# One query block of layer 0 scored once, queries on partitions, with DMA-turned weights

## The chip, the core and the metric

The kernel runs on one NeuronCore of a Trainium2 chip. Five engines work in parallel, each through its own queue of instructions in order: TensorE (PE, matmuls; PEld is its weight load), VectorE (DVE), ScalarE (ACT), GpSimd (POOL) and SyncE (SP), which here only starts DMA transfers. Engines wait for one another through semaphores. The metric is the device time of one execution in microseconds; the number to be predicted is the median of several executions.

## The reference, cut to what matters

Two layers over 1024 latent tokens and 256 context tokens of width 1024. Layer 0 is multi-head latent attention with 16 heads, layer 1 is differential attention with 8 head pairs. The change touches layer 0's attention only:

```python
def one_block(qb):                                   # q: 64 plain + 32 rotary columns a head
    s = jnp.einsum('bqhgd,bkhd->bhgqk', qb, k).astype(jnp.float32) * scale
    p = jax.nn.softmax(s, axis=-1).astype(v.dtype)
    return jnp.einsum('bhgqk,bkhv->bqhgv', p, v)

# latent queries see latent and context keys, context queries only context keys
o = dense_attention(q, concat([k, k_c]), concat([v, v_c]), scale)
o_c = dense_attention(q_c, k_c, v_c, scale)
```

Inputs are float32. The kernel keeps the precision by splitting operands into a high and a low half (float16 in the attention, a rounded float32 in the projections) and summing three products: high by high, high by low, low by high.

## The kernel before, in words

Before layer 0's attention the kernel computes modulation, input projections and gates (to about 222 us), and after it the output projection with layer norm, then layer 1 (from about 925 us) and its output.

Layer 0's attention is the function `heads0`. Each head has three chunks of queries (`CHUNKS`): b=0 is tokens 0 to 511, b=1 is tokens 512 to 1023, b=2 is the 256 context tokens. For a head and a chunk two things are done.

- `maxima0` finds a bound for the softmax. With queries on partitions it computes the high-by-high scores of each 128-query tile against all 1024 latent keys (`m.mm`, two matmuls of 512 columns into a PSUM pair, line 931), takes the row maximum on DVE (`m.max`, line 935), does the same for the 256 context keys (`m.mmc`, `m.maxc`, lines 942 and 947), joins both (`m.ng`), turns the 128 x 4 maxima into rows by a small matmul (`m.turn`, line 953) and writes them as four extra rows of the query tile `qH` (`m.row`, line 956). The key tile has the constant 16 in those rows, so a matmul over 100 rows subtracts the bound by itself.
- `attend0` computes the scores again, this time with keys on partitions and all three products (`s.mm`, six matmuls of 512 columns a unit, lines 980 to 982). A unit is two key tiles by 512 queries, one PSUM pair of 128 x 1024. Five units make a chunk (four of latent keys, one of context keys). ACT takes the exponential (`s.exp`, L986) and casts to float16 (`s.hi`, L988), POOL subtracts to get the low half (`s.lo`, L990), and because keys are on partitions the weights are already laid out for the second product: `pv.hi` (L998, L999) and `pv.lo` (L1005) add into one PSUM bank of kind "d" that is held for the whole chunk. Then DVE divides by the sum (`o.rc`, `o.out`, L1013, L1014) and SP stores the heads' output.

So the high-by-high product of every query chunk is computed twice, once in each orientation.

The PSUM holds three pairs (kind "a") for scores, maxima and projections, and two banks (kind "d") for results. The order of the work is written out by a planner (class `Plan`): each piece is a task with an engine, an estimated cost, buffers that it reads, writes and takes new, and a priority, which is a place on a scale of 11 units a head (`a`) plus an offset for its kind (`OFF0`). The planner runs the tasks through a model of the engines, picks on each engine among the tasks that could start first (within `EPS0`) the one of lowest priority, and looks no further than `AHEAD0` units ahead. The resulting order is what each engine's queue executes, SP's included. A new buffer of a kind takes the oldest of a ring: the n-th buffer back has to be free.

Around the heads: `query_move` and `key_move` bring a head's queries and keys to partitions 0 to 95 by SBUF-to-SBUF DMAs on SP (line 119; four transfers a query chunk, two for the keys). `key_pair`, `query_pair` and `turned` project for two or four heads at once and take the staging tiles `stk*`, `stq*`, `stp*`, `rsw`, `rr`. `range1` (lines 1025 to 1050, in head 2) computes layer 1's scale from small vectors, on DVE and with two small matmuls (L1035). `out_w0` loads the eight row blocks of the output weight in heads 14 and 15 into the two `ows` tiles and splits them (L1066 to L1068). In the last head the context chunk goes first, so that the context tokens' output projection (`ctx_turn`, `ctx_half`, L1092 and L219 to L221) can follow the last scores on PE.

Layer 1 treats a tile of 128 queries in another way, which is of use below: scores once with queries on partitions, maximum on DVE, the bound as the bias of the exponential (L1887), a cast and a subtraction (L1905, L1906), and then two DMA transposes on SP (`far.move`, L1909) that put keys on partitions for the second product (L1809 to L1811).

Of the kernel before, what the change touches and what calls it, by code (L numbers as in the profile page):

```python
# [14 lines left out]
ALU = mybir.AluOpType  # L15
# [18 lines left out]
PB = (3, 4)  # L34
# [28 lines left out]
OFF0 = {"c.hi": -13.45, "c.lo": -225.35, "c.load": 1.9, "c.mm": 1.45, "c.mul": -306.3, "c.turn": -151.55, "h.ab":  # L63
       26.55, "h.mm": -70.9, "h.three": 48.15, "h.two": -80.0, "k.hi": -179.3, "k.lo": 6.35, "k.mm": -8.55,
       "k.move": -44.05, "keep": -65.25, "m.max": -11.25, "m.maxc": -38.85, "m.mm": -1.15, "m.mmc": -1.55, "m.ng":
       -157.1, "m.row": -55.4, "m.turn": -102.05, "o.out": -258.15, "o.rc": -53.05, "o.store": -100.35, "open":
       -81.95, "p.add": 7.75, "p.c.hi": -140.45, "p.c.lo": -123.0, "p.cos": -56.4, "p.hi": -40.35, "p.lo": -17.55,
       "p.mm": -4.65, "p.mmc": 0.95, "p.sin": -19.1, "p.swap": -162.2, "pv.hi": 1.8, "pv.lo": 1.65, "q.hi": -104.55,
       "q.lo": -126.15, "q.mm": -5.3, "q.move": -151.4, "s.exp": -36.65, "s.hi": -13.6, "s.lo": -137.8, "s.mm":
       -0.75, "v.hi": 9.4, "v.lo": -112.0, "v.mm": -2.1, "v.out": 11.15, "v.sub": -65.0, "w.hi": 22.9, "w.lo":  # L70
       -226.85, "w.load": -135.85}
EPS0 = dict(P=0.0, A=0.0, D=0.15, G=0.3)
AHEAD0 = 30.25
# [13 lines left out]
def hybrid_kernel(  # L87
# [35 lines left out]

    def pair():

        return banks["pool"].tile([P, 1024], F32, tag="a", bufs=banks["a"], name=nm("ps_a"))
# [25 lines left out]
    ksc0, qsc0, esc0, sh0 = (col(1, s_) for s_ in ("ksc0", "qsc0", "esc0", "sh0"))  # L152
    ones = col(P, "ones")
# [267 lines left out]
    def up_weights(pa):  # L421
# [84 lines left out]
        dve.scalar_tensor_tensor(sh0, ksc0, math.log(4.0) / SC0, qsc0, op0=ALU.mult, op1=ALU.mult)  # L506
        kh_, kl_ = (u().bitcast(F16)[:ROPE, :NTOK] for _ in range(2))
# [93 lines left out]
    with spool("p0g") as pg:  # L601
# [18 lines left out]
        for _ in chain(gw, side):  # L620
# [13 lines left out]
            "qcL": ([100, 256], F16, 2), "op": ([P, NT, P], F32, 1), "mx": ([P, 4, 3], F32, 2),  # L634
            "ng": ([P, 4], F32R, 2), "rc": ([P, 4], F32, 2), "rsw": ([P, 1024], F32, 1), "rr": ([P, 1024], F32, 1),
            "stkH": ([P, NTOK], F16, 1), "stkL": ([P, NTOK], F16, 1), "stqH": ([P, NTOK], F16, 1),
            "stqL": ([P, NTOK], F16, 1), "stpH": ([P, NTOK], F16, 1), "stpL": ([P, NTOK], F16, 1),
            "ows": ([P, D], F32, 2), "cs": ([P, SEQ], F32, 2)}
    for k_, v_ in TAG0.items():
        rot(wk, v_[0], v_[1], k_, v_[2], first=True)  # L640
# [3 lines left out]
    rot(wk, *TAG0["p32"][:2], "p32", PB[0], first=True)  # L644

    def w0(tag, dt=None):
        sh, d, b = TAG0[tag]
        return rot(wk, sh, d, tag, b)

    cosA, sinA = w0("cs"), w0("cs")  # L650
# [38 lines left out]
    class Plan:  # L689
# [39 lines left out]

        def run(self, eps, ahead):  # L730
# [12 lines left out]
            order = []  # L743
            while done < len(T):
                best = None
                low = min(t["pri"] for l in ready.values() for t in l)
                for lim in (ahead, 1e9):
                    if best is not None:
                        break
                    for e, l in ready.items():  # L750
                        c = []
                        for t in l:
                            if t["pri"] > low + lim and t["pri"] > self.step + lim:
                                continue
                            st = max(free[e], t["at"])
                            if e == "G" or (e, t["kind"]) in self.PORT:
                                st = max(st, port)
                            for j, b in enumerate(t["new"]):
                                n, ring = self.rings[b.tag]
                                n -= sum(x.tag == b.tag for x in t["new"][:j])  # L760
                                if len(ring) >= n:
                                    for u in ring[-n].users:
                                        if u["end"] is None:
                                            st = None
                                            break
                                        st = max(st, u["end"] + self.LAT)
                                    if st is None:
                                        break
                            if st is not None:
                                c.append((st, t))  # L770
# [11 lines left out]
                for b in t["new"]:  # L782
                    self.rings[b.tag][1].append(b)
# [17 lines left out]
    def make0(tag):  # L801
        return pair() if tag == "a" else bank("d") if tag == "d" else w0(tag)
# [3 lines left out]
    def heads0():  # L806
# [3 lines left out]
        pl_ = Plan(rings, OFF0)  # L810
        add = pl_.add
# [151 lines left out]
        def attend0(h, b, a):  # L963
            c0, n = CHUNKS[b]
            QH, QLo = QT[h, b]
            kcs = list(range(0 if b < 2 else SEQ // P, NT, 2))
            nt = n // P
            nr = DQ + nt
            i = h % 2
            pv = new1("d")  # L970
            x = n == 512
            v_ = lambda: pv.tile[:, :4 * (V0 + 1)].rearrange("p (t d) -> p t d", t=4)
            for u, kc in enumerate(kcs):
                st, p32, ph, pl = new1("a"), new1("p32"), new1("ph"), new1("pl")

                def scores(kc=kc, st=st):
                    for j in range(2):
                        ks = slice((kc + j) * P, (kc + j + 1) * P)
                        s_ = st.tile[:, j * n:(j + 1) * n]
                        pe.matmul(s_, KH[i][:nr, ks], QH.tile[:nr, :], start=True, stop=False)  # L980
# [1152 lines left out]
```

## Time and profile before

| | us |
|---|---|
| median of 3 runs (1637.2 to 1639.33) | 1637.84 |
| profiled execution | 1638.62 |
| its span in the trace | 1636.8 |
| PE busy in the span | 1560.9 (95%) |
| DVE, ACT, POOL busy in the span | 1172.6, 1099.1, 1061.9 |
| PE's first and last score matmul of layer 0's attention (L980 start, L982 start) | 253.4, 721.4 |

The busy times are sums over instructions of one engine. PE's matmuls are pipelined, so that a busy PE can still have a few per cent to give; the exact cost of one more matmul in a full stretch is read from the chain of waits, where two matmuls of 512 columns take 0.43 us. "Chain" is the chain of work that ended last: followed back from the end, each instruction or the one that released it. Only what stands on it can shorten the kernel. The windows view gives for stretches of the span the busy time of each engine, PE's granted clock (1.00 is full speed) and the share of time in which the 16 DMA engines were busy.

### The profile page before, as it was taken

Reading aid. Unit: us, or ns where it says so; the run is one execution under the profiler, and the core shown is the slowest. Engines: PE = TensorE matmul, PEld = TensorE weight load, DVE = VectorE, ACT = ScalarE, POOL = GpSimd, SP = SyncE. Lnnn points to the kernel's source line nnn. Section 1 sums busy time; section 2 is a strip of 40 time slices with the busy share of each in tenths; the row PEclk is TensorE's granted clock in tenths of the full one; section 3 lists DMA queues with packets and bytes.
Section 4 is the critical chain, followed back from the end, with each engine's and each line's share of the span. In section 5 each row is a group of like instructions: output and inputs, shape, how many; then the busy total and the mean of one; then the engine's idle time right before and its main releaser. Section 6 shows DMA issues by size and latency. Waiting matters only on the chain.

```text
span 1636.8 us, 35530 instructions
## 1 busy us (share of the span) xinstructions
PE 1560.9 (95%) x13860; PEld 1135.9 (69%) x13860; DVE 1172.6 (72%) x1904; ACT 1099.1 (67%) x2074; POOL 1061.9 (65%) x816
## 2 busy tenths in 40 slices
PE   7999989999999999999999899999999999996998
PEld 6999965566666666667886576667676757574686
DVE  7757846776676676864774688888888888876763
ACT  2652147678878888974553678787878788867651
POOL 2513126767867877884556376877878687866794
PEclk9999999999999999999999999999999999997999
DMA  9347730111111102316443366667465666575772
GB/s 326 93 135 226 221 110 13 31 43 39 51 27 45 51 22 79 107 50 241 154 142 102 77 131 143 136 143 154 111 142 119 133 134 121 121 173 133 178 181 81
DMA packets 280438, 193.07 MB, mean 118 GB/s; under 512 B 181607, under 2 KB 255943, under 8 KB 280270
## 3 DMA queue, kind: packets, MB, share of 16 engines
q1 hardware_dynamic: 272398, 183.46, 44.2%
q10 hardware_dynamic: 7872, 7.34, 1.3%
q8 instruction: 109, 1.79, 0.5%
q14 instruction: 59, 0.48, 0.1%
HBM read 98.65 MB, written 27.07 MB: 77 GB/s over the span
## 4 chain that ended last, share of the span: by engine, by line
PE 65%; DVE 16%; DMA 5%; POOL 5%; ACT 5%; issue 3%; SPq 0%; POOLq 0%; DVEq 0%; ACTq 0%
PE ps_s L219 5%; PE ps_s L221 5%; PE ps_s L220 5%; PE ps_a L980 4%; PE ps_a L981 4%; PE ps_a L982 4%; PE ps_a L219 3%; PE ps_a L221 3%; PE ps_a L931 3%; PE ps_a L220 3%; DVE mx L1876 3%; DMA pd<-dl 2%; PE ps_d L998 2%; DVE p L1900 2%; PE ps_d L1005 2%
## 5 line engine op out<-in xcount | busy, mean ns | idle before, releaser
L990 POOL TENSOR_TENSOR pl<-p,ph 128x1024 f16<-128x1024 f32 (+1 forms) x176 | 362.1, 2076 | 113.7 <-ACT ph L988 79.3
L986 ACT ACTIVATE p<-ps_a,esc 128x1024 f32<-128x1024 f32 (+1 forms) x176 | 188.7, 1074 | 57.3 <-PE ps_a L982 42.8
L935 DVE TENSOR_REDUCE mx<-ps_a 128x1 f32<-128x1024 f32 x128 | 156.2, 1223 | 81.8 <-PE ps_a L931 81.1
L1906 POOL TENSOR_TENSOR dl<-p,dh 128x1280 f16<-128x1280 f32 x64 | 171.7, 2683 | 54.9 <-ACT dh L1905 35.5
L988 ACT CAST ph<-p 128x1024 f16<-128x1024 f32 (+1 forms) x176 | 176.5, 1006 | 9.7 <-PE ps_d L999 5.0
L1876 DVE TENSOR_REDUCE mx<-ps_p 128x1 f32<-128x512 f32 x256 | 163.9, 681 | 19.6 <-PE ps_p L1860 19.4
L1887 ACT ACTIVATE p<-ps_p,mx 128x512 f32<-128x512 f32 x256 | 173.3, 689 | 0.0
L1811 PE MATMUL ps_t<-vh,pd 128*128 128x128 f16 x640 | 113.2, 222 | 19.5 <-DMA pd<-dl 19.5
L980 PE MATMUL ps_a<-qH,KH 100*128 100x512 f16 x320 | 122.4, 382 | 2.1 <-ACT op L833 1.5
L981 PE MATMUL ps_a<-qH,KL 96*128 96x512 f16 x320 | 121.9, 381 | 0.0
L982 PE MATMUL ps_a<-qL,KH 96*128 96x512 f16 x320 | 121.0, 378 | 0.0
L1905 ACT CAST dh<-p 128x1280 f16<-128x1280 f32 x64 | 80.5, 1258 | 54.4 <-DVE p L1900 27.7
L1809 PE MATMUL ps_t<-vh,pd 128*128 128x128 f16 x640 | 113.8, 222 | 0.0
L1810 PE MATMUL ps_t<-vl,pd 128*128 128x128 f16 x640 | 113.6, 222 | 0.0
L1900 DVE SCALAR_TENSOR_TENSOR p<-p,sm,p 128x1280 f32<-128x1280 f32 x64 | 103.4, 1615 | 3.2
L998 PE MATMUL ps_d<-Vh,ph 128*128 128x65 f16 x1344 | 105.1, 195 | 0.0
L999 PE MATMUL ps_d<-Vl,ph 128*128 128x64 f16 x1344 | 104.6, 194 | 0.0
L998 PEld LDWEIGHTS <-ph 128*128 128x128 f16 x1344 | 90.3, 98 | 10.5 <-issue 5.3
L999 PEld LDWEIGHTS <-ph 128*128 128x128 f16 x1344 | 88.2, 98 | 4.5
L1887 ACT ACTIVATE p<-ps_c,mx 128x256 f32<-128x256 f32 x128 | 60.7, 474 | 33.7 <-DVE mx L1881 27.6
L1854 PE MATMUL ps_p<-KS,QS 128*128 128x512 f16 x256 | 77.2, 388 | 3.0 <-ACT p L1887 1.7
L1811 PEld LDWEIGHTS <-pd 128*128 128x128 f16 x640 | 63.5, 99 | 21.7 <-DMA pd<-dl 21.7
(496 smaller groups left out, 5115.9 us busy)
## 6 DMA issues: line engine op xcount, KB each, us to landing
ws<-in_dw SPq DMA_DIRECT2D x28, 512.0 KB, 4.9
adw<-in_ada_w SPq DMA_DIRECT2D x24, 512.0 KB, 4.7
adaw<-in_ada_w SPq DMA_DIRECT2D x16, 512.0 KB, 7.2
g<-sg_d SPq DMA_DIRECT2D x16, 512.0 KB, 4.4
sg_d<-gg ACTq DMA_DIRECT2D x40, 128.0 KB, 3.2
o_d<-op SPq DMA_DIRECT2D x7, 640.0 KB, 3.7
xt<-in_xT SPq DMA_DIRECT2D x16, 256.0 KB, 3.8
wgs<-in_w_in SPq DMA_DIRECT2D x32, 128.0 KB, 3.0
```

The costliest lines, as they stand in the source:

```text
L980: pe.matmul(s_, KH[i][:nr, ks], QH.tile[:nr, :], start=True, stop=False)
L981: pe.matmul(s_, KL[i][:DQ, ks], QH.tile[:DQ, :], start=False, stop=False)
L982: pe.matmul(s_, KH[i][:DQ, ks], QLo.tile[:DQ, :], start=False, stop=True)
L986: add("s.exp", "A", 1.114 if x else 0.682, lambda st=st, p32=p32: act.activation(p32.tile[:, :2 * n], st.tile[:, :2 * n], AF.Exp, scale=esc0),
L988: add("s.hi", "A", 1.046 if x else 0.618, lambda p32=p32, ph=ph: act.copy(ph.tile[:, :2 * n], p32.tile[:, :2 * n]), r=[p32], new=[ph], hol ...
L990: add("s.lo", "G", 2.14 if x else 1.17, lambda p32=p32, ph=ph, pl=pl: pool.tensor_tensor(pl.tile[:, :2 * n], p32.tile[:, :2 * n], ph.tile[ ...
L998: pe.matmul(v_()[:, t, :], w, Vh[:, k, h, :], start=(k == kcs[0] and t == 0), stop=False, skip_group_check=True)
L999: pe.matmul(v_()[:, t, :V0], w, Vl[:, k, h, :], start=False, stop=False, skip_group_check=True)
L1811: pe.matmul(pt.tile[:, :P], b, vh.tile[:, kc, :], start=False, stop=kc == NT - 1)
L1876: add(f"max{m}", "D", 0.68, lambda i=i, b_=b_: dve.tensor_reduce(mx.tile[:, 2 + 2 * m + i:3 + 2 * m + i], b_.tile, axis=AX.X, op=ALU.max, ...
L1887: add(f"exp{m}", "A", 0.78 if n == 512 else 0.57, lambda i=i, c0=c0, n=n, b=b, lo=lo: act.activation(p[m].tile[:, c0:c0 + n], b.tile[:, lo ...
L1906: add("far.lo", "G", 2.63, lambda: pool.tensor_tensor(dl.tile, p[0].tile, dh.tile, op=ALU.subtract), r=[p[0], dh], new=[dl], at=g + PR["fa ...
```

## The change

For chunk b=1 of each head the two functions are replaced by one, `mixed0`. For each of its four 128-query tiles it computes all three products once with queries on partitions (`x.mm`, six matmuls of 512 columns into a pair), takes the negated maximum (`x.max`), forms a bias of two small DVE instructions (`m.bias`), and takes the exponential with that bias (`x.exp`), the cast (`x.hi`) and the subtraction (`x.lo`) as before. Then two DMA transposes on SP (`s.turn0`, `s.turn1`) put the high and the low half, 128 x 1024 float16 each, with keys on partitions into one of the tiles `ows`, `rr`, `rsw`, and PE adds them into the result bank (`x.pvh`, `x.pvl`, as many matmuls as before). The context keys of the chunk are still done the other way round in one unit (`unit0`), with the bound written as rows of `qH` (`x.ng`, `x.trn`, `x.row`); their maximum (`x.mmc`, `x.maxc`, `m.cr`) now comes first.

Chunks b=0 and b=1 now alternate through the head (step 2.0 for both); before, b=0 came first. Layer 0's tiles and its PSUM pairs and banks get a tag for each buffer, and the planner picks among those that are free (`place`). There are five buffers of `ph` and `pl` in place of four, four of `mx`, three of `ng`. The output weight is loaded for all eight blocks in head 14 into `rr`, `rsw` and `cs`, after the point `open`, and the context loads (`c.load`) come after its splits. The planner's costs for `range1` rise (1.3 to 4.9, 0.52 to 1.1, 0.7 to 1.0), and all offsets, `EPS0` and `AHEAD0` (30.25 to 12.75) have new values.

```diff
-PB = (3, 4)
+PB = (3, 5)
-EPS0 = dict(P=0.0, A=0.0, D=0.15, G=0.3)
-AHEAD0 = 30.25
+EPS0 = dict(P=0.1, A=0.1, D=0.05, G=0.1)
+AHEAD0 = 12.75
...
+        def place(self, new):
+            st, taken = 0.0, []
+            for j, b in enumerate(new):
+                n, ring = self.rings[b.tag]
+                if self.pick:
+                    free = []
+                    for k, old in enumerate(self.held[b.tag]):
+                        us = old.users if old is not None else ()
+                        if (b.tag, k) not in taken and all(u["end"] is not None for u in us):
+                            free.append((max([u["end"] + self.LAT for u in us], default=0.0), k))
+                    if not free:
+                        return None
+                    at, k = min(free)
...
+        PDT = "ows", "rr", "ows", "rsw"
+        def mixed0(h, b, a, step=1.0):
...
+            add("x.mmc", "P", 4 * C(CTX), g, r=[(QH, "q"), KB[i]], new=[ps], at=a - 0.5)
+            add("x.maxc", "D", 1.223, lambda: dve.tensor_reduce(
+                mx.tile[:, :, 1], ps.tile.rearrange("p (a b) -> p a b", a=4), axis=AX.X, op=ALU.max, negate=True),
+                r=[ps], new=[mx], hold=1.255, at=a - 0.3)
+            add("m.cr", "D", 0.32, ctx_rows, w=[mx], new=[r16], hold=0.2, at=a - 0.25)
+            for t in range(4):
+                st, p32, ph, pl, pd = new1("a"), new1("p32"), new1("ph"), new1("pl"), new1("ows" if last else PDT[t])
+                def scores(st=st, ts=ts):
+                    for w, ks, first, stop in ((QH, KH, True, False), (QH, KL, False, False), (QLo, KH, False, True)):
+                        for c in range(2):
+                            pe.matmul(st.tile[:, c * 512:c * 512 + 512], w.tile[:DQ, ts], ks[i][:DQ, c * 512:c * 512 + 512], start=first, stop=stop)
+                def bias(t=t):
+                    dve.tensor_scalar(r16.tile[:, t:t + 1], mx.tile[:, t, 0:1], 1.0 / MROW0, sh0m, op0=ALU.mult, op1=ALU.add)
+                    dve.tensor_scalar(mx.tile[:, t, 2:3], r16.tile[:, t:t + 1], mx.tile[:, t, 1:2], esm0, op0=ALU.min, op1=ALU.mult)
...
+                add("x.exp", "A", 1.114, lambda t=t, st=st, p32=p32: act.activation(p32.tile, st.tile, AF.Exp, bias=mx.tile[:, t, 2:3], scale=esc0),
+                    r=[st, (mx, ("b", t))], new=[p32], hold=1.0, at=a + step * t + 0.3)
...
+                for j, d in enumerate((ph, pl)):
+                    add(f"s.turn{j}", "S", 3.4, lambda j=j, d=d, vw=vw: sp.dma_start_transpose(vw()[:, j], d.tile),
+                        r=[d], w=[(pd, 1)] if j else [], new=[] if j else [pd], hold=1.32, at=a + step * t + (0.9, 1.5)[j])
...
+            unit0(h, b, a + step * 4, 4, 4, 8, pv, False, True)
+            finish0(h, b, a, step * 5, pv)
...
-            ws = new1("ows")
-            add("w.load", "S", 3.90, lambda: ..., new=[ws], hold=0.42, at=a)
+            ws = new1(("rr", "rsw", "cs", "cs")[k % 4])
+            add("w.load", "S", 3.90, lambda: ..., r=[OPEN], new=[ws], hold=0.42, at=a)
...
-            maxima0(h, 1, g)
-            attend0(h, 0, g + 1.0 * last)
+            attend0(h, 0, g + 1.0 * last, 2.0)
-                attend0(h, 1, g + 5.0)
+                mixed0(h, 1, g + 1.0, 2.0)
...
-            if h >= H0 - 2:
-                for k in range(4):
-                    out_w0(4 * (h - H0 + 2) + k, g + 2.4 * k)
+            if h == H0 - 2:
+                for k in range(KT):
+                    out_w0(k, g + 1.3 * k)
```

More of the change, by code (lines that the diff above doesn't have):

```diff
@@ L122, in bank @@
         return banks["pool"].tile([P, 512], dt, tag=tag, bufs=banks[tag], name=nm("ps_" + tag))
+    pairs = []
     def pair():
[L126 removed]
+        return banks["pool"].tile([P, 1024], F32, tag=f"a{pairs.pop(0)}", bufs=1, name=nm("ps_a"))
     def spool(name, **kw):
@@ L757, in run @@
                                 st = max(st, port)
[L758 to L768, printed above, removed]
+                            if t["new"]:
+                                got = self.place(t["new"])
+                                st = None if got is None else max(st, got[0])
                             if st is not None:
@@ L1167, in heads0 @@
                 for b in t["new"]:
-                    b.tile = make0(b.tag)
+                    b.tile = make0(b.tag, b.slot)
                 t["f"]()
+        pairs.extend([k for k in range(3) if k not in (y8.slot, y9.slot)] + [y8.slot, y9.slot])
         yctx[8] = [y8.tile[:, :512], y8.tile[:, 512:]]
```

215 lines of the change are left out of this document (147 added, 68 removed).

## The prediction

> **What bounds the kernel now.** I read the windows view first (start:end, length, then busy us and instructions in brackets of PE, PEld, DVE, ACT, POOL, then PE's granted clock, DMA share, GB/s). Its rows are a disturbed part of layer 0's attention, nearly all of that attention, and layer 1.
>
> ```profile
> 285.00:315.00 30.00, 26.86 (x304) 16.95 (x302) 22.15 (x36) 19.81 (x19) 21.63 (x11) 0.89 0.09 23
> 255.00:705.00 450.00, 446.22 (x5449) 292.85 (x5448) 314.77 (x425) 368.29 (x374) 336.33 (x166) 0.99 0.17 47
> 1000.00:1500.00 500.00, 471.74 (x4059) 321.15 (x4056) 413.10 (x792) 398.73 (x987) 385.41 (x347) 0.99 0.64 136
> ```
>
> From 255 to 705 PE is idle for 450 − 446.2 = 3.8 us; no other engine comes near. The chain of waits (start, us, what) agrees: from head to head it is PE's own work. Its maxima matmuls return with a period of four heads (the projection `turned` comes every fourth head), so two rows give the time of a head, and the cost of what the change removes:
>
> ```profile
> 450.55 0.43 PE ps_a L931 x2
> ...
> 569.40 0.43 PE ps_a L931 x2
> ```
>
> (569.40 − 450.55) / 4 = 29.7 us a head, and 0.43 us on the chain for two maxima matmuls of 512 columns, 0.215 each. Layer 0's attention is bound by PE's instruction stream. The grouped instructions (count, busy us, mean ns) give the other prices:
>
> ```profile
> L990 POOL TENSOR_TENSOR pl<-p,ph 128x1024 f16<-128x1024 f32 (+1 forms) x176 | 362.1, 2076 | 113.7 <-ACT ph L988 79.3
> L986 ACT ACTIVATE p<-ps_a,esc 128x1024 f32<-128x1024 f32 (+1 forms) x176 | 188.7, 1074 | 57.3 <-PE ps_a L982 42.8
> L935 DVE TENSOR_REDUCE mx<-ps_a 128x1 f32<-128x1024 f32 x128 | 156.2, 1223 | 81.8 <-PE ps_a L931 81.1
> L988 ACT CAST ph<-p 128x1024 f16<-128x1024 f32 (+1 forms) x176 | 176.5, 1006 | 9.7 <-PE ps_d L999 5.0
> L931 PE MATMUL ps_a<-KH,qH 96*128 96x512 f16 x256 | 76.2, 379 | 1.8 <-DVE Vl L836 1.4 <-ACT op L833 0.4
> L1879 DVE TENSOR_SCALAR mx<-mx 128x1 f32<-128x1 f32 x128 | 34.9, 273 | 4.7
> L1881 DVE TENSOR_SCALAR mx<-mx,lcf 128x1 f32<-128x1 f32 x64 | 13.7, 214 | 2.3
> ```
>
> **The change, part by part.** *Removed on PE:* half of L931's 256 matmuls, that of chunk b=1: 16 heads × 8 = 128 × 0.215 = **−27.5 us**, all on the chain. Nothing is added on PE in exchange: `x.mm` is six matmuls of 512 columns for each of four query tiles where `s.mm` was six for each of four key pairs; `x.pvh` and `x.pvl` are 24 a tile as before; `x.mmc` and `x.trn` take the place of `m.mmc` and `m.turn`.
>
> *What covers the other engines.* A head should then take 29.7 − 1.7 = 28.0 us. ACT has the same instructions: 368.29 / 450 × 29.7 = 24.3 us a head, 87% of 28.0. POOL 336.33 / 450 × 29.7 = 22.2, 79%. DVE keeps its 1.22 us maxima and gains ten small instructions a head (`m.bias` two a tile, `m.cr` two), at the two small rows above 4 × (0.273 + 0.214) + 2 × 0.214 = 2.4 us: 314.77 / 450 × 29.7 + 2.4 = 23.2, 83%. So I cost them at nothing as work; if PE's cover failed, ACT's 24.3 would be the next floor.
>
> *Added on SP and the DMA engines:* eight transposes a head, 128 in all. Layer 0 has none; layer 1 has them at 128 x 1280. The first row gives the issue time on SP (min/median/max ns), the second the time from issue to landing, the next two are windows in which one such transpose was nearly alone, then two query moves on SP and what PE waited for in layer 1:
>
> ```profile
> L1909 SPq DMA_TRANSPOSE pd<-dh x64: 1252/1340/2694, 929.1 to 1583.5; - x64
> ...
> DMA to landing us min/median/max: 3.3/3.4/5.7
> ...
> 1136.00:1137.00 1.00, 1.00 (x10) 0.90 (x10) 1.00 (x2) 0.34 (x1) 1.00 (x2) 1.00 0.92 178
> 1137.00:1138.00 1.00, 1.00 (x12) 0.89 (x11) 1.00 (x3) 0.92 (x1) 0.83 (x4) 1.00 0.80 150
> ...
> 447.92 0.51 SPq L119 DMA_DIRECT2D qH<-stqH  x1
> ...
> 449.40 0.55 SPq L119 DMA_DIRECT2D qL<-stqL  x1
> ...
> PE ps_t L1811 <- DMA pd<-dl: 15.5, 9, 4.9
> PE ps_c L1848 <- ACT p L1887: 12.2, 8, 4.1
> ```
>
> SP's queue: 8 × 1.34 + 14 moves × 0.55 = 18.4 us a head, 66% of 28.0. The DMA engines: 0.92 + 0.80 = 1.72 us of all sixteen for 1280 columns, 1.38 for 1024; 8 × 1.38 + 0.17 × 28 = 15.8 us, 56%, below layer 1's 0.64. Neither is a floor, but both are queues in order: a transpose that waits for POOL's `x.lo` holds back the next head's `query_move`, and with that the first `x.mm` or `m.mm` that reads it.
>
> *The longer way of a query tile.* Between scores and second product now stand also the maximum 1.22, the bias 0.49 and the landing 3.4: **5.1 us more**. The pair is held by a tile for 6 × 0.215 + 1.22 + 0.49 + 1.07 = 4.1 us; before, a maxima pair (0.43 + 1.22) and a score pair (1.29 + 1.07) made 4.0. So the three pairs get no fuller. The two "d" banks do: with b=0 and b=1 alternating, both are open through most of a head, and b=2 needs one in between. What PE loses by waiting, the trace of before doesn't show for layer 0. From below it is its own idle time, 3.8 − 3.1 us (the 3.1 is explained below) or 0.01 us for each of the 64 tiles. From above it is layer 1, where every tile goes this way: 28.3 us idle in 500, and its 64 tiles start from 929.1 to 1583.5, 10.2 us each, so 49 tiles and 0.58 us a tile, 37 us for 64. I take 0.08, **+5.0 us**: near the lower end, because here a head has, beside the four tiles, seven other score units, the next head's maxima and the projections, which need no transpose.
>
> *`range1` in head 2.* PE's wait, the DVE chain that caused it, and one-us windows:
>
> ```profile
> PE ps_a L1035 <- DVE hm L1030: 3.1, 1, 3.1
> ...
> 301.31 1.16 DVE cols L572
> 302.49 2.05 DVE ab L574
> 304.65 1.98 DVE ab L576
> ...
> 306.00:307.00 1.00, 0.00 (x0) 0.00 (x0) 0.97 (x5) 0.00 (x0) 0.61 (x1) 0.89 0.00 0
> 307.00:308.00 1.00, 0.79 (x4) 0.82 (x5) 1.00 (x3) 0.00 (x0) 0.00 (x0) 0.50 0.00 0
> ...
> 312.00:313.00 1.00, 1.00 (x3) 0.29 (x2) 0.00 (x0) 0.00 (x0) 1.00 (x1) 0.50 0.00 0
> 313.00:314.00 1.00, 1.00 (x9) 0.44 (x8) 0.00 (x0) 0.00 (x0) 0.65 (x1) 0.70 0.00 0
> ```
>
> The plan held this DVE piece for 1.3 us; it took 5.8 (301.31 to 307.1), so PE's order put the small matmul too early: 3.1 us idle, then a clock of 0.50 from 307 to 313 and 0.70 to 314, another 6 × 0.5 + 0.3 = 3.3. With the cost at 4.9 the order leaves at most 0.9 us uncovered, too short a gap to look like this one: 6.4 − 0.9 = **−5.5 us**. Bounds: −6.4, and 0 if the new order finds no other PE work while DVE, now in the way of every tile's exponential, is blocked.
>
> The Trainium skill, "TensorE: Matmul & The Clock Gate", section "Why this matters for your kernels", warns of PE idle for more than about 3 us between bursts, since the clock then falls to half. The trace agrees: 3.1 us idle, then 0.50. By that rule a wait for a late transpose costs double once it is that long, and this speaks against the change; the rival it makes stands below.
>
> *The end of the attention.* Before, the last units ran like this; the windows show PE full, then 4 − 2.28 = 1.7 us idle:
>
> ```profile
> 717.16 1.12 ACT p L986
> 718.30 1.05 ACT ph L988
> 719.39 2.48 POOL pl L990
> ...
> 720.00:724.00 4.00, 3.90 (x82) 3.09 (x77) 3.94 (x4) 3.51 (x5) 4.00 (x2) 1.00 0.02 4
> 724.00:728.00 4.00, 2.28 (x39) 2.07 (x40) 0.90 (x2) 2.96 (x4) 4.00 (x3) 1.00 0.22 66
> ```
>
> Now the last query tile's way is 5.1 us longer, and it holds an `ows` tile that the context's `ctx_turn` needs. One score unit (1.3 us) can follow it on PE: 5.1 − 1.3 = **+3.8 us**; bounds 0, if the order puts the tiles ahead of b=0's units, and 5.1. The eight weight loads in head 14 I cost at nothing: ACT and DVE do the same splits as before, and PE doesn't wait for them until `ctx_half`.
>
> *Sum*, against the profiled execution: 1638.6 − 27.5 + 5.0 − 5.5 + 3.8 = 1614.4. That execution lies 0.8 us above the median of the runs, so the median should be **1614 us**.
>
> **The rivals.** *All of it comes:* no new waits, `range1` wholly covered, the end hidden: 1638.6 − 27.5 − 6.4 − 0.8 = 1604. For it: the pairs are no fuller, and PE before lost 0.01 us a tile. Against it: two engines at 83 and 87% stand in a chain that PE must wait out.
>
> *Half of layer 1's waits:* 64 × 0.29 = 18.6, and 5.1 at the end: 1638.6 − 27.5 − 5.5 + 18.6 + 5.1 − 0.8 = 1628. For it: DVE would be at 83% and ACT at 87%, in layer 1 they are at 83% and 80% with PE at 94%. Against it: less of PE's work here depends on transposes.
>
> *One long stall in head 14,* where transposes share the queue with eight loads of 512 KB. Layer 1 has such a place, its chain entry first:
>
> ```profile
> 1488.25 8.12 DMA pd<-dl
> ...
> 1490.00:1492.00 2.00, 1.53 (x7) 0.25 (x6) 1.97 (x2) 2.00 (x3) 2.00 (x1) 0.70 0.91 261
> 1492.00:1494.00 2.00, 0.00 (x0) 0.00 (x0) 1.90 (x3) 0.91 (x2) 0.22 (x2) 1.00 1.90 189
> 1494.00:1496.00 2.00, 0.00 (x0) 0.00 (x0) 1.93 (x5) 1.57 (x3) 0.00 (x0) 0.66 0.62 171
> 1496.00:1498.00 2.00, 1.58 (x16) 1.58 (x16) 2.00 (x2) 1.50 (x6) 1.49 (x1) 0.50 1.08 330
> ...
> 1506.00:1508.00 2.00, 2.00 (x8) 0.33 (x7) 0.40 (x1) 0.39 (x1) 2.00 (x2) 0.50 0.00 0
> ```
>
> Idle 0.47 + 2 + 2 + 0.42 = 4.9 us, then half clock from 1496 to 1508, 6 more: 11 us, 1614 + 11 = 1625. The skill's page named above would expect just this pair of costs.
>
> *Slower:* PE waits for each tile as in layer 1, at the place where `x.pvh` and `x.pvl` want a transposed tile or the exponential holds the pair: 64 × 0.58 = 37.1, and 5.1 at the end: 1638.6 − 27.5 − 5.5 + 37.1 + 5.1 − 0.8 = 1647. It decides from (27.5 + 5.5 − 3.8) / 64 = 0.46 us a tile. For it: it is the only measured price of this chain. Against it: in layer 1 no engine is full, so that gaps are nobody's loss to fill; here PE has some 20 us of other work a head (28.0 less 4 × 1.29 for the tiles' scores and their second products).
>
> *It doesn't do what it says:* the time of a head is not PE's, and 28.0 can't be reached because ACT's 24.3 with its waits already fills it: 1638. Against it, PE's 3.8 us idle.
>
> **How the numbers follow.** Forecast 0.49 (its own range 1608 to 1621), all of it 0.15, half of layer 1's waits 0.16, the long stall 0.06, slower 0.10, no effect 0.04. Below 1602 and above 1634 I leave about 0.04 and 0.16. A measurement of this kernel tells about 0.2%, 3.3 us, from no change. Faster: 0.49 + 0.15 + 0.16 + 0.06 = 0.86; same 0.04; slower 0.10.
>
> **What would show it.** In the profile after: L931's kind at 128 instead of 256 matmuls; score and maxima lines back on the chain with a head of about 28 us; PE idle in the attention below some 6 us beside the end; no clock of 0.50 in head 2; transposes that land in about 3.4 us; PE's waits for `pd` short and scattered. I am wrong if PE is idle by more than 0.2 us a tile, if SP's order makes moves late so that PE waits for queries, or if ACT or DVE lines replace PE on the chain.

## The result, and the profile after

| | us |
|---|---|
| before, median of 4 runs (1637.13 to 1639.33) | 1637.52 |
| after, median of 4 runs (1679.62 to 1691.82) | 1684.92 |
| ratio, 95% interval | 1.029 (1.025 to 1.033) |
| profiled execution of after, its span | 1683.6, 1681.7 |

The change made the kernel 47 us slower where 23 us less were forecast. The windows view by stage shows where it lost most: the attention of layer 0 from its first to its last score matmul, and the stretch from the end of the context's output product to layer 1's first score. First the kernel before, then after (columns as in the prediction: stretch, length, busy us and instructions of PE, PEld, DVE, ACT, POOL, granted clock, DMA share, GB/s).

```profile
253.40:721.80 468.40, 464.60 (x5666) 304.02 (x5666) 329.54 (x441) 384.59 (x390) 354.68 (x173) 0.99 0.18 48
752.10:914.50 162.40, 155.71 (x873) 122.06 (x872) 95.17 (x133) 84.77 (x168) 86.52 (x74) 0.99 0.43 142
```

```profile
253.40:763.00 509.60, 462.58 (x5532) 302.26 (x5531) 400.15 (x599) 384.87 (x393) 355.01 (x174) 0.95 0.59 109
798.30:967.70 169.40, 156.12 (x874) 122.83 (x874) 99.45 (x135) 85.53 (x169) 90.99 (x78) 0.97 0.46 151
```

PE has its 128 matmuls less, but the attention is 41 us longer: PE is idle for 509.6 − 462.6 = 47 us in place of 4, and its mean clock is 0.95. VectorE is busy for 400 us where 330 were needed before. The second stretch is 7.0 us longer with the same work. Between the two the context's output product ends 5.0 us later after the last score (35.3 us against 30.3), and layer 1 is 8 us shorter with the same instructions, which stays unexplained (last section). PE's waits in after's attention (line waited for: us in total, times, longest) name VectorE above all, transposes for only 2.1 us in layer 0; the four largest rows:

```profile
PE ps_a L1104 <- DVE mx L983: 11.3, 6, 3.0
PE ps_d L1139 <- DVE ng L1137: 6.9, 7, 1.4
PE ps_d L1133 <- DVE qH L1142: 6.7, 2, 3.3
PE ps_a L978 <- DVE stkL L895: 6.3, 4, 2.1
```

VectorE's groups of small instructions in layer 0 of after (count, busy us, mean ns) show what is late:

```profile
L1090 DVE CAST mx<-r 128x4 f32<-128x4 f16 x16 | 24.6, 1540 | 0.6
L1108 DVE TENSOR_SCALAR mx<-r,mx,esm 128x1 f32<-128x1 f16 x64 | 17.5, 273 | 2.3
L1137 DVE TENSOR_TENSOR ng<-r,mx 128x4 fp32r<-128x4 f16 x16 | 17.3, 1083 | 0.0
L1089 DVE TENSOR_SCALAR r<-mx,sh0m 128x4 f16<-128x4 f32 x16 | 16.6, 1039 | 0.5
L1107 DVE TENSOR_SCALAR r<-mx,sh0m 128x1 f16<-128x1 f32 x64 | 13.4, 210 | 0.8
```

The one-column forms take 0.21 and 0.27 us, as forecast. The three four-column ones (`m.cr` in L1089 and L1090, `x.ng` in L1137), which handle only four numbers a partition, take 1.0 to 1.5 us each on the average. The chain of waits of after (start, us, what) and one row of GpSimd's timeline over the same place, three subtractions run together:

```profile
444.81 0.74 DVE qH L992
445.58 1.24 DVE mx L1093
446.84 0.61 DVE r L1089
447.48 2.05 DVE mx L1090
449.53 1.12 DVE mx L1112
450.66 0.61 DVE mx L983
451.31 1.46 PE ps_a L1104 x6
```

```profile
444.17 5.33 POOL L1042 TENSOR_TENSOR pl<-p,ph 128x1024 f16<-128x1024 f32 x3
```

The cast `mx` of L1090 ends at 449.53, at the moment when GpSimd's run of subtractions ends (444.17 + 5.33 = 449.50). Behind it on VectorE wait the two maxima that PE's score pairs are held for, so PE gets its next pair only at 451.31.

What the forecast had priced from the trace is there: the transposes of after on SP (min/median/max ns) and their landing:

```profile
L1122 SPq DMA_TRANSPOSE ows<-ph x34: 1232/1239/2045, 260.1 to 763.7; - x34
...
DMA to landing us min/median/max: 3.0/3.3/5.9
```

### The profile page after: what moved, and what is told of

It reads as the page before. It is cut to its first block, busy times and chain, and to the rows that moved or that the text cites. A ratio compares the mean times of both kernels' runs of the same rounds, so it can differ in the third digit from the quotient of the medians.

```text
span 1681.7 us, 35639 instructions
## 1 busy us (share of the span) xinstructions
PE 1559.5 (93%) x13732; PEld 1136.1 (68%) x13732; DVE 1249.1 (74%) x2066; ACT 1096.1 (65%) x2074; POOL 1059.4 (63%) x816
## 4 chain that ended last, share of the span: by engine, by line
PE 59%; DVE 24%; DMA 5%; ACT 4%; issue 4%; POOL 2%; SPq 0%; DVEq 0%; POOLq 0%; ACTq 0%
PE ps_s L223 6%; PE ps_s L225 5%; PE ps_s L224 5%; PE ps_a L1104 4%; PE ps_a L223 3%; DVE mx L2002 3%; PE ps_a L225 3%; PE ps_a L224 3%; PE ps_a L1032 2%; PE ps_a L1033 2%; PE ps_a L1034 2%; DVE p L2026 2%; DMA pd<-dl 2%; PE ps_p L1980 2%; DVE mx L1112 2%
## 5 line engine op out<-in xcount | busy, mean ns | idle before, releaser
L1042 POOL TENSOR_TENSOR pl<-p,ph 128x1024 f16<-128x1024 f32 (+1 forms) x112 | 226.7, 2028 | 102.8 <-ACT ph L1040 67.7
L1118 POOL TENSOR_TENSOR pl<-p,ph 128x1024 f16<-128x1024 f32 x64 | 137.1, 2149 | 52.5 <-ACT ph L1117 33.1
L1038 ACT ACTIVATE p<-ps_a,esc 128x1024 f32<-128x1024 f32 (+1 forms) x112 | 117.8, 1051 | 73.5 <-PE ps_a L1034 55.5
L1040 ACT CAST ph<-p 128x1024 f16<-128x1024 f32 (+1 forms) x112 | 110.0, 983 | 2.1
L1115 ACT ACTIVATE p<-ps_a,mx,esc 128x1024 f32<-128x1024 f32 x64 | 76.9, 1202 | 47.2 <-DVE mx L1108 46.1
L1032 PE MATMUL ps_a<-qH,KH 100*128 100x512 f16 x192 | 77.3, 402 | 7.0 <-ACT p L1115 4.1
L1033 PE MATMUL ps_a<-qH,KL 96*128 96x512 f16 x192 | 77.3, 402 | 0.0
L1034 PE MATMUL ps_a<-qL,KH 96*128 96x512 f16 x192 | 76.5, 398 | 0.0
L1937 PEld LDWEIGHTS <-pd 128*128 128x128 f16 x640 | 63.1, 99 | 17.0 <-DMA pd<-dl 16.8
L1935 PEld LDWEIGHTS <-pd 128*128 128x128 f16 x640 | 63.0, 98 | 9.6 <-issue 6.4
```

The costliest lines, as they stand in the source:

```text
L1038: add("s.exp", "A", 1.114 if x else 0.682, lambda st=st, p32=p32: act.activation(p32.tile[:, :2 * n], st.tile[:, :2 * n], AF.Exp, scale=esc0),
L1042: add("s.lo", "G", 2.14 if x else 1.17, lambda p32=p32, ph=ph, pl=pl: pool.tensor_tensor(pl.tile[:, :2 * n], p32.tile[:, :2 * n], ph.tile[ ...
L1118: add("x.lo", "G", 2.14, lambda p32=p32, ph=ph, pl=pl: pool.tensor_tensor(pl.tile, p32.tile, ph.tile, op=ALU.subtract), r=[p32, ph], new=[ ...
L1935: pe.matmul(pt.tile[:, :P], a, vh.tile[:, kc, :], start=kc == 0, stop=False)
L1937: pe.matmul(pt.tile[:, :P], b, vh.tile[:, kc, :], start=False, stop=kc == NT - 1)
```

## The experiments

The theory formed from this profile: the four-column instructions wait for GpSimd, and that is the loss. Its rivals: the transposes and their queue, the planner's choice of buffers, the longer chain of a tile. Times are medians, with the ratio to the kernel before and its 95% interval.

### Taking the wait away

*e1_free_small:* the context's row in four one-column instructions, the two other four-column ones as reductions of the same numbers. `R16()` is the tile `r16` with its eight columns as four pairs, so that one reduction can join the two values of a tile; `m.bias` writes its columns in the same layout.

```diff
-dve.tensor_scalar(r16.tile[:, 4:8], mx.tile[:, :, 1], 1.0 / MROW0, sh0m, op0=ALU.mult, op1=ALU.add)
-dve.tensor_copy(mx.tile[:, :, 1], r16.tile[:, 4:8])
+for t in range(4):
+    dve.tensor_scalar(R16()[:, t, 1:2], mx.tile[:, t, 1:2], 1.0 / MROW0, sh0m, op0=ALU.mult, op1=ALU.add)
+dve.tensor_reduce(mx.tile[:, :, 1], R16()[:, :, 1:2], axis=AX.X, op=ALU.max)
...
-dve.tensor_tensor(ng.tile, r16.tile[:, :4], mx.tile[:, :, 1], op=ALU.min)
+dve.tensor_reduce(ng.tile, R16(), axis=AX.X, op=ALU.min)
```

> The changed kernel with its small DVE instructions in forms that read SBUF through one port only: the tensor_scalar of 128x4 becomes four of 128x1, the cast and the minimum of two SBUF tensors become tensor_reduce. The order on every engine stays, and so does what is computed. Theory A (these three wait for GpSimd's running subtraction, 58.5 us on DVE in the changed kernel, and hold up the maxima behind them, so PE idles and its clock falls): they shrink to about 20 us, and of the 47 us that were lost 25 to 55 come back: 1630 to 1660 us. Theory B (the new order with its transposes and alternating chunks stalls PE by itself): within 5 us of 1685.

*e3_cr_free* has the first half of this edit alone (`m.cr`, both its lines), *e6_ng_free* the second (`x.ng`).

> The changed kernel with only the context rows (m.cr) in the free form; the joined bound (x.ng) stays a tensor_tensor of two SBUF tensors. If the loss is shared as the waits on DVE are (41 us for m.cr, 17 for x.ng), 54 x 0.7 = 38 of the 54 us come back: about 1647. If x.ng alone is the one that PE waits for (17 us of waits in the changed kernel's list for the small matmul behind it), 1660 or more.

> The changed kernel with only the joined bound (x.ng) in the free form; the context rows (m.cr) stay as in the change. If the loss is shared as the waits on DVE are, about 1669. If x.ng is the one that counts, 1650 or less. If the two losses don't add (the clock falls only where both fall together), the two runs together give back clearly more or less than 54 us.

Measured: e1 **1630.75**, 0.9957 (0.9937 to 0.9976); e3 1647.99, 1.0055 (1.0037 to 1.0074); e6 1665.6, 1.0164 (1.0134 to 1.0195). From 1684.9 the first edit gives back 37 us, the second 19, both together 54: within the intervals they add up. The rows of e1, in the order of the edit:

```profile
L1091 DVE TENSOR_SCALAR r<-mx,sh0m 128x1 f16<-128x1 f32 x64 | 9.3, 210 | 0.5
L1092 DVE TENSOR_REDUCE mx<-r 128x4 f32<-128x4 f16 x16 | 2.5, 159 | 0.6
L1139 DVE TENSOR_REDUCE ng<-r 128x4 fp32r<-128x8 f16 x16 | 2.4, 150 | 0.0
```

Three times 16 instructions took 58.5 us in after; 96 take 14.2 here. So the form of three tiny instructions made most of the loss.

### What they wait for

*e8_halves:* the changed kernel, with GpSimd's subtraction of 1024 columns written as two of 512.

```diff
-pool.tensor_tensor(pl.tile, p32.tile, ph.tile, op=ALU.subtract)
+for c in range(0, 1024, 512):
+    pool.tensor_tensor(pl.tile[:, c:c + 512], p32.tile[:, c:c + 512], ph.tile[:, c:c + 512], op=ALU.subtract)
```

> The changed kernel with GpSimd's subtraction of each 128x1024 score block written as two instructions of 128x512 (1.15 us each by the context's rows, where one of 1024 takes 2.15 to 2.17); nothing else, the other four engines keep their instructions and order. Theory (a four-column instruction of VectorE waits until the GpSimd instruction that is running has ended): the longest wait becomes one short instruction, so the cast's maximum falls from 2.13 us to about 1.2 and its mean from 1.54 to 0.7 to 0.9, the two others' in the same proportion; of the 54 us that taking the waits away gave, about half comes back, less what GpSimd's longer work (0.14 us in each of 160 blocks) takes: 1660 (1650 to 1672). Rival 1 (VectorE waits for a result of GpSimd or for the whole subtraction, or falls behind the next half too): mean and maximum as before, 1685 or over. Rival 2 (the instructions are slow by themselves, whatever GpSimd does): mean as before, 1683 to 1690.

Measured: **1639.11**, 1.000 (0.998 to 1.002). First after, then e8 (ns min/median/max of the same instructions):

```profile
L1090 DVE CAST mx<-r x16: 170/2056/2126, 254.1 to 738.0; 128x4 f32<-128x4 f16 x16
L1137 DVE TENSOR_TENSOR ng<-r,mx x16: 158/1492/2090, 270.1 to 757.8; 128x4 fp32r<-128x4 f16 x16
```

```profile
L1094 DVE CAST mx<-r x16: 171/1082/1092, 254.0 to 690.2; 128x4 f32<-128x4 f16 x16
L1141 DVE TENSOR_TENSOR ng<-r,mx x16: 152/581/1171, 270.1 to 707.2; 128x4 fp32r<-128x4 f16 x16
```

The longest wait goes from the length of one subtraction of 1024 columns (2.15 us) to that of one of 512 (1.18): here VectorE waits until the GpSimd instruction that is running has ended. The shortest, 0.15 to 0.17 us, is the instruction's own cost. The Trainium skill, "SBUF — State Buffer", section "Who interferes with whom", states this: VectorE and GpSimd share a pair of SBUF ports under an exclusive lock, which casts and `tensor_scalar` in their two-port modes and any VectorE instruction with two SBUF inputs need and reductions don't; the loser "fully blocks". The traces agree (2.06 us for the cast, 0.16 for the reduction). The expected 1660 was wrong: half of the waiting time gave back 46 of the 54 us. So the loss isn't in proportion to the waits. In e8's attention (253 to 710 us) PE is idle for 18.8 us where after has 47, no gap of PE is longer than 2 us, and the granted clock stays at 1.00. That a wait of 1.1 us mostly finds a score pair still ahead of PE, and one of 2.1 doesn't, fits this but isn't shown.

### The transposes and the choice of buffers

*e2_plain_copy:* the low halves are copied, not transposed (the second product then uses unturned low halves, so this kernel leaves out part of the computation).

```diff
-sp.dma_start_transpose(vw()[:, j], d.tile)
+sp.dma_start(pd.tile.bitcast(F16)[:, 1024:2048], d.tile) if j else sp.dma_start_transpose(vw()[:, 0], d.tile)
```

> The changed kernel with the low halves' 64 transposes replaced by plain copies of the same 256 KB, in the same order; the low halves reach the second product unturned, so the output isn't the reference's. Theory A (small DVE instructions): within 5 us of 1685. Theory B in the form that transposes land late or fill SP's queue: half of that cause is gone, 15 to 30 us back, 1655 to 1670.

*e4_pick_alone:* the kernel before, with a tag for each buffer and the planner picking among the free ones (`place`), nothing else of the change.

> The kernel before with only one part of the change: layer 0's buffers and PSUM banks get a tag each and the planner picks among the free ones; old scores, old offsets. Theory A: no effect, 1634 to 1640. Rival (the free choice makes new waits or breaks a good order): 1642 or more.

*e5_range_cost:* the kernel before, with the raised costs of `range1` alone.

```diff
-add("h.ab", "D", 1.3, first_, w=[HM], at=a)
-add("h.mm", "P", 0.52, spread, r=[HM], new=[bk], at=a + 0.5)
-add("h.two", "D", 0.7, second, r=[bk], w=[HM], at=a + 0.7)
+add("h.ab", "D", 4.9, first_, w=[HM], at=a)
+add("h.mm", "P", 1.1, spread, r=[HM], new=[bk], at=a + 0.5)
+add("h.two", "D", 1.0, second, r=[bk], w=[HM], at=a + 0.7)
```

> The kernel before with only the planner's costs of range1 raised as in the change (1.3 to 4.9, 0.52 to 1.1, 0.7 to 1.0). The prediction's term of -5.5 us: 1630 to 1634, with no clock of 0.50 in head 2. Rival (the order shifts, and the 5 us DVE piece stalls PE all the same): 1637 to 1643.

Measured: e2 1680.57, 1.0268 (1.0229 to 1.0308), some 4 us below after with overlapping intervals, so a transpose in place of a plain copy, for half of them, isn't seen to cost anything here; e4 1635.59, 0.9989 (0.9971 to 1.0007); e5 1637.16, 0.9998 (0.9979 to 1.0016). Neither part moves the time alone. On e5 its rival holds: in its trace the piece of `range1` still takes 8 us (301.2 to 309.2), three of its eight-column instructions taking 2.0 to 2.1 us each, and the clock is still 0.62 to 0.69 from 310 to 320.

### The order of the work

*e7_replan:* e1 with the planner told what e1's trace shows, and all offsets, `EPS0` and `AHEAD0` chosen anew. *e9_before_replan:* e4 with the same chosen anew. In both the planner counts two more VectorE pieces, `c.mul` and `h.ab`, as shut out by GpSimd. The costs that e7 changes, in part:

```diff
-add("m.cr", "D", 0.32, ctx_rows, w=[mx], new=[r16], hold=0.2, at=a - 0.25)
+add("m.cr", "D", 1.05, ctx_rows, w=[mx], new=[r16], hold=1.0, at=a - 0.25)
...
-add("m.bias", "D", 0.32, ..., hold=0.2, at=a + step * t + 0.25)
+add("m.bias", "D", 0.5, ..., hold=0.45, at=a + step * t + 0.25)
```

> The version with only single-column and reduce forms in the block statistics, its order planned anew: the planner is told what its trace shows for the block's row statistics (1.0 us instead of 0.2 for the context's row, 0.45 instead of 0.2 for a tile's bias, 1.09 instead of 1.0 for the exponential with a bias, 1.27 for a transpose's issue), counts two more of VectorE's operations as shut out by GpSimd, and its offsets are chosen for these costs; the same work on every engine. Theory (what is left of waits comes from an order planned with costs too low): in that version's trace the stretch 253 to 735 us has 466.5 us of TensorE's work in 482.0 us, so 15.5 us idle where the kernel before has 6.0 in 477.0; an order that fits brings the idle time down to about 6 us: some 9 us less than its 1630.8, 1622 (1616 to 1627). Rival (the idle time belongs to the longer chain of each tile, scores to maximum to bias to exponential to two transposes, whatever the order): within 3 us of 1630.8.

> The control for the newly planned order: the kernel before, with its layer 0 buffers picked among the free ones and its order planned anew in the same way, the same work on every engine as before. If the kernel before has as little left in its order as its 6 us of idle TensorE between 253 and 730 us say, it gains no more than 0 to 5 us: 1632 to 1638. If a new plan by itself is worth 9 us or more, this version shows it too, 1629 or less, and what the newly planned change wins is not the change's.

Measured: e7 **1640.67**, 1.001 (0.999 to 1.003), 10 us worse than e1; e9 **1629.03**, 0.994 (0.993 to 0.996). Both expectations on e7 missed. e9 gained 9.7 us, more than its theory's 0 to 5: it stands at the bound of its rival, by which a new order by itself is worth 9 us or more. Attention of e1, of e7, of e9:

```profile
254.80:708.50 453.70, 441.71 (x5537) 291.70 (x5537) 358.38 (x648) 382.05 (x392) 356.24 (x174) 1.00 0.67 122
```

```profile
253.40:710.40 457.00, 441.52 (x5505) 289.17 (x5504) 356.87 (x626) 383.95 (x390) 354.90 (x171) 1.00 0.64 118
```

```profile
253.40:710.80 457.40, 457.37 (x5616) 297.94 (x5616) 313.86 (x416) 383.39 (x390) 354.82 (x172) 1.00 0.19 52
```

In the kernel before, with the old way of computing, a better order fills PE to the last 0.03 us. In the changed kernel 12 to 15 us stay idle in either order that was tried; in e7 PE's longest waits there are for transposes that are issued between query moves (its chain: `309.66 4.76 DMA ows<-pl`). Of e7's 10 us the attention shows only 3; most of the rest comes behind it, before layer 1 begins (920.5 − 710.4 = 210.1 us against e1's 912.1 − 708.5 = 203.6). That an order exists that fills the 12 us isn't excluded.

### A wait behind the attention

After and e1 have one more wait that before has not, where the tokens' output begins. The chain of e1 there, and the same place in PE's and SP's waits:

```profile
742.25 0.24 PE ps_d L224
742.50 0.02 issue
742.51 0.32 SPq L1411
742.83 0.04 issue
742.88 4.62 DMA g<-sg_d
...
747.66 2.35 POOL o L1415
```

```profile
PE ps_a L687 <- POOL o L1415: 7.3, 1, 7.3
...
SPq L1411 <- PE ps_d L224: 17.8, 1, 17.8
```

SP stands for 17.8 us at the load of the first attention output `o`, until the context's output product has ended, and PE then waits 7.3 us. In the kernel before this load went out at 737.5, 14.6 us ahead of that product's end. The change made the rings `ph` and `pl` one buffer deeper, 2 KB a partition each; all later buffers of layer 0 move up by 4 KB or a little more, and `rr`, which the context's last product reads to its end, comes to lie under the next stage's `o`.

*e10_rr_moved:* e1 with four small buffers behind `rr` in the layout instead of ahead of it. *e11_before_pad:* the kernel before with an unused 4 KB ahead of layer 0's buffers. Both have the same instructions in the same order as the kernel that they start from.

```diff
-"qcH": ([100, 256], F16, 2), "qcL": ([100, 256], F16, 2), "op": ([P, NT, P], F32, 1), "mx": ([P, 4, 3], F32, 4),
-"ng": ([P, 4], F32R, 3), "rc": ([P, 4], F32, 2), "rsw": ([P, 1024], F32, 1), "rr": ([P, 1024], F32, 1),
+"op": ([P, NT, P], F32, 1), "ng": ([P, 4], F32R, 3), "rsw": ([P, 1024], F32, 1), "rr": ([P, 1024], F32, 1),
+"qcH": ([100, 256], F16, 2), "qcL": ([100, 256], F16, 2), "mx": ([P, 4, 3], F32, 4), "rc": ([P, 4], F32, 2),
```

```diff
-TAG0 = {"ph": ([P, 1024], F16, PB[1]), ...
+TAG0 = {"pad": ([P, 1024], F32, 1), "ph": ([P, 1024], F16, PB[1]), ...
```

> The version with only single-column and reduce forms in the block statistics, with four small buffers of layer 0 (qcH, qcL, mx, rc: 2368 bytes a partition together) laid out after rr instead of ahead of it; same instructions, same order on all engines. With its two rings of probability halves one buffer deeper, the change has moved every later buffer of layer 0 up by 4 KB and more; the buffer rr, which holds a turned half of the context's last tile and is read to the end of layer 0's context output product, now lies under the first attention-output tile o of the next stage. In that version's trace SyncE's load of o waited 17.8 us for TensorE's last product there (until 742.5 us), and TensorE then waited 7.3 us for GpSimd's product of o, with 10.2 us at the half clock behind it; in the trace before the load went out at 737.5, 14.6 us ahead of the product's end. Theory (the wait is the layout's): with rr under a buffer that is needed later the load goes out by about 725, the 7.3 us wait goes, and about 3 us of the half clock: 1630.8 less 7 to 12, 1621 (1618 to 1625). Rival (the load is late for another reason, or the weights' load behind it, 13.9 us, sets the end anyway): within 3 us of 1630.8.

> The kernel before with a buffer of 4 KB a partition put ahead of layer 0's others and never used: the same instructions in the same order, rr moved by 4 KB under o as the change moved it. Theory (the layout alone costs): the first load of o waits for the context product's end, TensorE waits some 7 us for o there and runs some microseconds at the half clock: 7 to 12 us slower, 1646 (1643 to 1650). Rival (it is not the layout): 1635 to 1640. It also tells whether layer 1, whose instructions are the same in all kernels and which took 677.4 to 683.1 us in the four traces without the change and 671.3 to 675.9 in the seven with it, goes by the layout: then it comes out below 676 here.

Measured: e10 **1615.57**, 0.987 (0.985 to 0.989); e11 **1650.3**, 1.0067 (1.0051 to 1.0083). The load of `o` on SP in e10, and in e11 with PE's wait behind it:

```profile
719.12 0.38 SPq L1411 DMA_DIRECT2D o<-o_d  x1
```

```profile
752.42 0.32 SPq L1283 DMA_DIRECT2D o<-o_d  x1
...
PE ps_a L676 <- POOL o L1287: 7.6, 1, 7.6
```

The layout alone costs the kernel before 11 us (against 1639.5 in the same comparison), and giving it back wins 15 in the changed one, more than the 7 to 12 expected. e10 is the best kernel here: 1.3% below the kernel before. But e9 had 0.6% by a new order alone, so what the change itself is worth beside a kernel whose order was also chosen anew is some 0.7%, 12 us (ratios 0.987 and 0.994).

*e12_moved_halves:* e10 with e8's two half subtractions.

> The version with rr moved, and GpSimd's 1024-column subtractions written as two of 512. The statistics no longer wait for GpSimd there; left are VectorE's two-input instructions of the last two heads: the output weights' low parts took 2.13 to 2.66 us each and the context's gating products 3.0 to 3.1, against 1.45 for the shortest of the one and 2.2 of the other with halves. Theory (these waits still lengthen layer 0's end): up to 8 x 0.9 + 2 x 0.9 = 9 us less VectorE work there, of which the end sees about a third: 2 to 4 us below the version without halves. Rival (GpSimd's 0.14 us more in each of 160 blocks is paid instead, since the low halves' transposes wait for it): the same or up to 4 us above it.

Measured: 1620.31, 0.989 (0.987 to 0.990), 5 us above e10; the rival holds in its sign. The output weight's low parts did get shorter, but one of the context's gating products of e12 did not get in at all while GpSimd's short instructions followed one another (VectorE's row, then GpSimd's, start and us first):

```profile
708.68 7.51 DVE L1212 TENSOR_TENSOR rsw<-rsw,rr 128x1024 f32<-128x1024 f32 x1 [4.41 <-DMA rsw<-o_d]
...
699.46 15.64 POOL L698 TENSOR_TENSOR pl<-p,ph 128x512 f16<-128x512 f32 x14
```

It took 7.5 us where e10's took 2.4, and ended 1.1 us after GpSimd's series (716.2 and 715.1). So the wait is for the running instruction or for a whole series without a gap; which of the two decides isn't settled here.

## Why the prediction was wrong

**The step that failed** is the one on the ten small VectorE instructions: "2.4 us ... So I cost them at nothing as work". It priced all of them by L1879 and L1881, one-column forms, which took 0.21 to 0.27 us here too. The two of `m.cr` have four columns and took 41.2 us in all; a third, `x.ng`, isn't priced at all (before, `m.ng` is a reduction of 0.16 us) and took 17.3. They don't only take VectorE's time: `m.cr` stands in front of the maxima that free PE's pairs, and PE itself waits for `x.ng` at L1139. Together they cost **54 us** (e1). The trace of before held the warning: the prediction quoted `ab` of L574 at 2.05 us and L576 at 1.98 and took them for work. The next rows of before's timeline have the same two lines again, 2 us later:

```profile
306.55 0.15 DVE L574 TENSOR_TENSOR ab<-lng,cols 128x8 f32<-128x8 f32 x1
306.82 0.17 DVE L576 TENSOR_TENSOR ab<-ab,cols 128x8 f32<-128x8 f32 x1
```

An instruction of eight columns that takes 2.05 us once and 0.15 the next time has waited; GpSimd ran three subtractions from 300.30 to 306.61 there, and the second long one ends with them. The planner of both kernels knows such waits, too: its set `PORT` lists VectorE pieces that it keeps apart from GpSimd's, and `m.cr` and `x.ng` are not on it.

**The step that was missing** is the layout: the change part by part passes over "five buffers of `ph` and `pl` in place of four". It cost **15 us** (e1 to e10), in a stage that the diff doesn't touch. 1614 + 54 + 15 = 1683, against 1684.9; as both prices are read from e1 and e10, this says no more than that e10 came out 1.6 us from the forecast, and the terms below show that as luck.

**The other steps**, against e10, where neither stands in the way. First e10's attention and, after the comma of the second row, the start of its first score matmul of layer 1; then the same row of the kernel before:

```profile
252.00:704.20 452.20, 440.18 (x5537) 290.93 (x5537) 354.96 (x648) 381.67 (x392) 355.68 (x174) 1.00 0.68 123
...
L1982 PE MATMUL ps_p<-KS,QS x256: 376/379/634, 898.9 to 1549.9; 128*128 128x512 f16 x128
```

```profile
L1854 PE MATMUL ps_p<-KS,QS x256: 376/379/650, 914.5 to 1566.5; 128*128 128x512 f16 x128
```

- *PE's −27.5 us:* right. Counted from each matmul's start to the next, those of the maxima take 51.8 us in before's stretch (L931, 246) and 25.0 in e10's (120), 26.8 less. PE's busy time fell by only 464.6 − 440.2 = 24.4 us, although the half clock of `range1` (3.3 by the prediction) is gone too: "Nothing is added on PE in exchange" was not quite so. The second products take 124.6 us in place of 120.1 by the same count; the rest isn't traced here.
- *The waits, +5.0 (0.08 us a tile):* PE is idle for 12.0 us there, 8.2 more than before. With the 3.1 us of `range1` gone, 0.7 was to become 5.7; so the waits cost 11.3 us, 0.18 us a tile, more than twice the term.
- *`range1`, −5.5:* the costs alone don't bring it (e5). In e10 no half clock shows at that place, and the eight-column `ab` instructions no longer wait (0.16 to 0.17 us each), but what it gained can't be read apart from the rest of the new order.
- *The end of the attention, +3.8:* from the last latent score to the end of the context's product 36.6 us (704.2 to 740.8) in place of 30.3 (721.8 to 752.1), +6.3.
- *The transposes on SP and the DMA engines, nothing:* issue 1.24 and landing 3.3 us (medians), against 1.34 and 3.4 taken. PE waits 5.7 us in all for them in e10, most of it within the 12.0 above.
- All terms lie ahead of layer 1's first score, and together they are −24.2 us; up to there e10's trace saves 15.6 (914.5 to 898.9). Of this, 4.3 us come from the stretch behind the context's product (158.1 us in place of 162.4), for which the forecast had no term. The execution that left this trace took 1622.0 us, the other three of e10 1614.8 to 1615.7; where these save the rest, of 22 to 24 in the median, no trace shows. So the sum's nearness to e10's 1615.6 is not a sign that its terms were right.

**The rivals.** "Slower" had the right sign with 0.10, at the wrong place: it had PE waiting for transposed tiles, or for an exponential that holds the pair, 37 us, and in layer 0 of after PE waited 2.1 us in all for transposes. Waits of this kind are part of what remains in e10, where all of PE's idle time is less than half of the 0.46 us a tile that the rival needed to decide. "Half of layer 1's waits", 1628, came close to e1's time by another sum. The clock did what the prediction had seen in `range1`, and more often: in after's attention it falls to 0.50 eleven times, for 3.4 or 6.8 us each. PE's busy time for the same matmuls is 462.6 us there and 441.7 in e1, some 21 of the 54 us. The prediction let a wait cost double once it is about 3 us long; here shorter ones did it too: the clock falls at 422.6 behind two gaps of 1.3 and 1.1 us, and once in e1's attention, at 661.6, where no gap of PE is longer than 1.8.

## What to carry to other kernels

Price a small VectorE instruction by a row of the same form, columns and operands, not by its size; where GpSimd works on SBUF all the time, write tiny statistics as one-column or reduce instructions, and look for long durations of small tiles in the trace of before. When a change adds buffers, ask which later stage's tiles come to lie on which of the moved ones, and who reads those last. If a change whose arithmetic is sound comes out slower, undo its smallest parts first: 48 instructions and 4 KB of layout hid a kernel that is 1.3% faster. And give the old kernel the same new order before calling the gain the change's: here that takes about half of it away.

## What was not expected of the hardware

- The same four numbers a partition cost 0.16 us as a reduction and 2.06 us (median) as a cast beside GpSimd's 2.1-us subtractions; 1.08 beside subtractions of 1.18 us.
- Halving the waits gave back 85% of what they cost (46 of 54 us), and with no gap of PE over 2 us the clock stayed at 1.00.
- An exponential with a bias of its own for each partition took 1.20 us for 128x1024 (x64, after), where one without takes 1.11.
- Layer 1, from its first score to its last second product, took 671 to 683 us in fourteen traces, with the same instructions. In e1 and the other kernels with the change, e10 aside, it is 671.3 to 676.6, without the change 677.4 to 683.1; but e10 has 678.5, and e11, which has the change's layout at that place, 680.1. What sets it stays open; a difference of a few microseconds between two single traces is no result.
